# Cross-attention queries by a seven-product scheme, with the sample's padded queries kept for two chunks at a time

## The chip, the cores and the metric

The kernel runs on one core of a Trainium2 chip. The metric is the time of one execution on the device, in microseconds, as the median of several runs; smaller is better. The engines are named as in the profile: PE is the matrix engine (TensorE) and PEld its weight loads, DVE is VectorE, ACT is ScalarE, POOL is GpSimd, SP is the engine whose queue issues most of the transfers.

## The reference

One inference step of a decoder layer, for a prompt of 512 tokens and a sample group of 8 sequences with 8 tokens each, with the same weights; the model has 1024 channels, and all is float32.

```python
x = x + 0.5 * swiglu(rmsnorm(x, ffn1_norm), ffn1_w_gate, ffn1_w_up, ffn1_w_down)
h = rmsnorm(x, mix_norm);  u_lru, gate, u_pool = split(h @ w_in)
x = x + concat(gelu(gate) * rglru(conv(u_lru)), pool_mixer(u_pool)) @ w_out
x = x + cross_attend(rmsnorm(x, xattn_norm), mem_k, mem_v, xattn_wq, xattn_wo)
x = x + 0.5 * swiglu(rmsnorm(x, ffn2_norm), ffn2_w_gate, ffn2_w_up, ffn2_w_down)
y = rmsnorm(x, final_norm)

def cross_attend(h, k, v, wq, wo):                     # 4 heads of 256, 256 memory tokens
    q = (h @ wq).reshape(b, t, 4, 256)
    p = softmax(einsum('bthd,bmhd->bhtm', q, k) / 16)
    return einsum('bhtm,bmhd->bthd', p, v).reshape(b, t, 1024) @ wo
```

For the prompt, `mem_k` and `mem_v` are computed from the normed memory; for the sample they are inputs (a cache of 8 sequences x 256 tokens).

## The kernel before, in words

Activations lie transposed: 8 chunks (`DC`) of 128 channels, each 128 partitions x 576 tokens (512 of the prompt, 64 of the sample), in two halves of 288 (`HT`). Each float32 operand of a matmul is kept as a high part, rounded to the fp32r type by ScalarE (`split`, L182), and a low part, the rest, formed by VectorE (L185 or L187). A product takes three matmuls: high x high, high x low, low x high (`mm3`, all matmuls recorded at L139).

`project` takes one output chunk of 128 channels by all 8 input chunks: 8 x 3 x 2 halves = 48 matmuls of 288 columns. A weight panel (512 KB) goes through `panel`: a load into one of six `wr` buffers (L192), then the high and low part in one of four `wh` and four `wl` buffers each.

The feed-forward parts use another scheme, which the change brings to the queries. Two output chunks by two input chunks by two halves of the tokens form a 2 x 2 block product; it is done as seven block products (`product`, 12 matmuls of 288 columns each over four pairs of input chunks) on sums of weight blocks (`E`, `F`, `G`, `H` beside the plain `11`, `12`, `22`) and sums of the operand's blocks (`T1` to `T4` beside `N11`, `N21`, `N22`). `HalfNorm` keeps that operand: seven blocks of 288 for each pair of chunks, high and low; `sums` makes `T1` to `T3`, `last` makes `T4`. The accumulators `U`, `A`, `C` are read out between the products.

The stages around the change, in order:

- the output projection (`w_out`, tile `wo`): 8 panels; after each chunk the residual is added (L1250), and `nx.add` splits the new `x` into the operand `nx` of the queries and sums its squares. The squares of the memory tokens (`mem`) are summed meanwhile, and `mem` is normed and split into `mh`, `ml` (L1261).
- the memory keys (`mem_k`, tile `k`): 8 panels of 24 matmuls of 256 columns, results split into `kk` and sent out. The factor `r` of the norm is made after the third.
- the queries (`query`, tile `q`): 8 panels by `project`. `query_out` scales the result by `r` (L1278), splits the prompt's columns into `qq`, and copies the sample's columns to `z` (L1281), which is filled with zeros elsewhere, so that a matmul with it gives one head's scores at its rows.
- after every second chunk `sample_scores` multiplies the two chunks before with the cached keys: four loads of 512 KB (`ck`, L1300) into two `wh` and two `wl` buffers, and four small matmuls with each key (tile `ss`, L1302; each appears as two in the trace).
- then the values (`mem_v`), the last pair's sample scores, the softmax, and so on.

The order on each engine is made by a scheduler that takes the earliest ready instruction of the program; a buffer that comes free goes to the earliest tile that asks for it. Within the feed-forward parts (`"ff" in now`) the matmuls are chained in the program's order; in the rest they are not.

Of the kernel before, what the change touches and what calls it, by code (L numbers as in the profile page):

```python
# [16 lines left out]
P = 128  # L17
# [29 lines left out]
XH, HD = 4, 256  # L47
EPS = 1e-6


# [18 lines left out]
def hybrid_step(ctx, tc, a):  # L69
# [34 lines left out]
    def col(name, i=0):  # L104
        c = _C[name] + i
        return cst[:, c:c + 1]
# [10 lines left out]
    neg = const.tile([P, 2, DC], F32, name="neg")  # L117
    for i, name in enumerate(("g1", "g2")):
        v.tensor_scalar(neg[:, i, :], cst[:, _C[name]:_C[name] + DC], -1.0, None, op0=ALU.mult)

    def ncol(name, i=0):
        return neg[:, ("g1", "g2").index(name), i:i + 1]

# [5 lines left out]

    chain, latest = [None], [None]  # L130

# [5 lines left out]
    def mm(*args, **kw):  # L137

        i = te.matmul(*args, **kw)  # L139
# [1082 lines left out]

    nx = Norm("gx", "nx", now["r1"])
    xp = begin("xa")
    if True:
        def xtemp(n, name):
            return xp.tile([P, n], F32, tag="q", bufs=3, name=name)

        mem = xp.tile([P, DC, ML], F32, tag="B8", bufs=3, name="mem")
        nc.sync.dma_start(mem, a["memT"])  # L1230
        macc = xp.tile([P, ML], F32, name="macc")

        def mem_square(j):
            if j == 0:
                s.activation(macc, mem[:, j, :], AF.Square)
            else:
                sq = rows.tile([P, ML], F32, tag="sq", name="msq")
                s.activation(sq, mem[:, j, :], AF.Square)
                v.tensor_add(macc, macc, sq)

        wos = []
        for j in range(DC):
            wos.append((bank(f"wo{j}"), panel(a["w_out"][j], DC, P, "o", freed if j else None)))

            project(*wos[j], yy, range(LC, DC), last=False)
            if j < 2:
                continue
            for i in range(3) if j == 2 else (j,):
                project(*wos[i], yy, range(LC), first=False)
                v.tensor_add(halves(x[:, i, :]), wos[i][0][:, :, :HT], halves(x[:, i, :]))  # L1250
                nx.add(i)
            for i in range(3 * j - 6, min(3 * j - 3, DC)):
                mem_square(i)
            background()
            if j == 5:
                mq = row_factor([macc], "mem", wos[j][0][:, 1, :], ML)
            if j == 6:
                mr = spread(mq, "mem", ML)
                mh, ml = (xp.tile([P, DC, ML], F32R, tag="B8", bufs=3, name=f"m{q}") for q in "hl")
                for i in range(DC):  # L1260
                    v.scalar_tensor_tensor(out=mem[:, i, :], in0=mem[:, i, :], scalar=col("gk", i), in1=mr,  # L1261
                                           op0=ALU.mult, op1=ALU.mult)
                    split(mh[:, i, :], ml[:, i, :], mem[:, i, :])
# [6 lines left out]
        qs = {}  # L1270
# [5 lines left out]
        def query_out(j):  # L1276
            q = xtemp(T, f"q{j}")
            v.tensor_mul(halves(q), qs[j][:, :, :HT], halves(r))  # L1278
            split(qq[0][:, j, :TP], qq[1][:, j, :TP], q[:, :TP])
            h = j // 2  # L1280
            v.tensor_copy(z[:, :, j, h * ST:(h + 1) * ST], q[:, TP:].rearrange("p (b k) -> p b k", k=ST))  # L1281

        def mem_k(j):
# [5 lines left out]
            split(kk[:, 0, j, :], kk[:, 1, j, :], ps[:, 0, :ML])  # L1289
            o = xtemp(ML, f"ko{j}")  # L1290
            s.copy(o, ps[:, 0, :ML])
            nc.scalar.dma_start(a["o_k"][:, j, :], o)
            return ps

        def sample_scores(*js):

            for j in js:
                for g in range(2):
                    t = wp.tile([P, 4, ML], F32, tag=("wh", "wl")[g], name=f"ck{g}{j}")
                    nc.sync.dma_start(t, a["ck"][g, j])  # L1300
                    for b in range(4):
                        te.matmul(sps[b * 32:(b + 1) * 32, g, :ML], lhsT=z[:, 4 * g + b, j, :], rhs=t[:, b, :],  # L1302
                                      start=j == 0, stop=j == DC - 1)
# [12 lines left out]

        vv = now["r1"].tile([P, 2, 2, XH * HD], F32R, tag="A", bufs=2, name="vv")
        at = now["r1"].tile([P, DC * T], F32, tag="A", bufs=2, name="at")
        prob = [at[:, i * 4 * ML:(i + 1) * 4 * ML].rearrange("p (t n) -> p t n", n=ML) for i in range(2)]
        c0 = 8 * ML  # L1320
        pst = at[:, c0:c0 + 2 * ML].rearrange("p (g n) -> p g n", n=ML)
        pss = at[:, c0 + 2 * ML:c0 + 4 * ML].rearrange("p (g m n) -> p g m n", g=2, m=2)
        so = [at[:, c0 + (4 + i) * HD:c0 + (5 + i) * HD] for i in range(4)]

        def mem_v(h):
# [106 lines left out]
        mem_v(0)()  # L1432
        sample_scores(DC - 2, DC - 1)
        softmax(pst, sps[:, :, :ML], 2, "s")
# [32 lines left out]
        first[0] = None  # L1467
        end("xa")
        n2 = HalfNorm("g2", "n2", begin("s2"))
# [35 lines left out]
def _inputs(i):  # L1505
# [105 lines left out]
```

## Time and profile before

| | |
|---|---|
| median of 3 runs | 1124.35 us (1122.2 to 1124.86) |
| profiled execution, first to last instruction | 1120.1 us; no other time is given for it |
| TensorE busy, granted clock | 1104.7 us (99%), 0.997 |
| VectorE busy | 859.0 us (77%) |
| ScalarE busy | 669.7 us (60%) |
| queries, from the first q matmul to the last | 556.08 to 613.43 us |

Matmuls are pipelined and the row's mean duration of one is longer than their spacing, so the time of a group is read from the chain of waits: its rows are start, length, engine and tile, and number of instructions, in us. A row of a group of instructions is: line, engine, operation, output <- inputs, shapes, count | busy us, mean ns | idle time of the engine just before, and what ended it. A row of a stretch of time is: from:to, length, then for PE, PEld, DVE, ACT and POOL the busy us and the count of instructions, then the granted clock, the share of the DMA engines and GB/s.

### The profile page before, as it was taken

The page shows a single profiled execution, that of the slowest core. Times are in us where ns is not written, and L with a number is a line of the kernel's source. Part 1 is how long each engine was busy: PE and PEld are TensorE (multiplying, and loading weights), DVE is VectorE, ACT ScalarE, POOL GpSimd, SP SyncE. Part 2 cuts the span into 40 slices and gives each one's busy share as a digit, 9 for nine tenths or more (in the row PEclk, how much of TensorE's full clock was granted, in tenths as well). Part 3 has the DMA queues.
Part 4 walks back from the last instruction along what each step waited for, and adds up shares of the span by engine and source line. Part 5 has one row for each costly group of instructions (what it writes and reads, how often), then busy time and mean ns, then how long its engine had stood idle before and what let it go on. Part 6 is the DMA issues. An engine that isn't in the chain of part 4 may idle for free.

```text
span 1120.1 us, 21943 instructions
## 1 busy us (share of the span) xinstructions
PE 1104.7 (99%) x8430; PEld 1087.3 (97%) x8430; DVE 859.0 (77%) x1535; ACT 669.7 (60%) x1262; POOL 191.9 (17%) x232
## 2 busy tenths in 40 slices
PE   8999999999999999999999999999999999999997
PEld 8999999999999999999999889999999999999996
DVE  7899888889865878977733666779879888787754
ACT  8566666666664645765712455446667666666554
POOL 0012222221221024422000000000222222222111
PEclk9999999999999999999999999999999999999998
DMA  9457777776766656567656862233786777877652
GB/s 327 112 132 177 156 161 166 168 174 147 165 142 141 196 150 135 118 187 168 194 202 211 302 202 85 76 98 76 166 183 150 184 171 164 187 156 164 143 111 85
DMA packets 95257, 180.15 MB, mean 161 GB/s; under 512 B 9968, under 2 KB 47856, under 8 KB 95024
## 3 DMA queue, kind: packets, MB, share of 16 engines
q1 hardware_dynamic: 61024, 124.68, 35.0%
q0 software_dynamic: 31472, 51.65, 28.4%
q10 hardware_dynamic: 2656, 2.41, 0.7%
q8 instruction: 66, 1.08, 0.4%
q14 instruction: 39, 0.32, 0.1%
HBM read 140.87 MB, written 13.20 MB: 138 GB/s over the span
## 4 chain that ended last, share of the span: by engine, by line
PE 93%; DVE 3%; DMA 2%; issue 1%; ACT 1%; SPq 0%; POOL 0%; POOLq 0%; DVEq 0%; ACTq 0%
PE pu L139 22%; PE pc L139 10%; PE dU L139 9%; PE pd L139 6%; PE pa L139 5%; PE xo L139 5%; PE q L139 5%; PE wo L139 5%; PE pg L139 3%; PE in_l L139 2%; PE in_p L139 2%; PE in_g L139 2%; PE dA L139 2%; PE dD L139 2%; PE dC L139 2%; PE k L139 2%
## 5 line engine op out<-in xcount | busy, mean ns | idle before, releaser
L465 POOL DMA_DIRECT2D r<-f_gu x39 | 35.0, 897 | 425.3 <-DVE r L462 261.5
L182 ACT CAST dh<-td 128x512 fp32r<-128x512 f32 x96 | 59.3, 618 | 30.9 <-PE dA L139 12.2
L139 PE MATMUL dU<-ph,dh 128*128 128x288 f32 x256 | 75.7, 296 | 0.7 <-ACT add L651 0.7
L139 PE MATMUL dU<-ph,dl 128*128 128x288 f32 x256 | 75.4, 295 | 0.0
L139 PE MATMUL dU<-pl,dh 128*128 128x288 f32 x256 | 75.4, 295 | 0.0
L185 DVE TENSOR_TENSOR dl<-td,dh 128x512 fp32r<-128x512 f32 x96 | 64.6, 685 | 10.2 <-ACT dh L182 10.0
L185 DVE TENSOR_TENSOR wl_e<-r,wh_e 128x1024 fp32r<-128x1024 f32 x39 | 47.6, 1222 | 27.1 <-ACT wh_e L182 27.1
L667 POOL DMA_DIRECT2D x<-add_e x32 | 38.9, 1215 | 146.2 <-ACT add_e L651 43.5
L182 ACT CAST wh_g<-r 128x1024 fp32r<-128x1024 f32 x39 | 41.0, 1051 | 26.8 <-DVE r L481 14.1
L694 POOL DMA_DIRECT2D x<-add x32 | 31.3, 980 | 135.9 <-ACT add L651 91.0
L185 DVE TENSOR_TENSOR wl_h<-r,wh_h 128x1024 fp32r<-128x1024 f32 x39 | 47.6, 1220 | 3.0 <-ACT wh_h L182 3.0
L139 PEld LDWEIGHTS dU<-ph,dh 128*128 128x128 f32 x256 | 48.1, 188 | 1.2 <-ACT add L651 1.2
L139 PEld LDWEIGHTS dU<-ph,dl 128*128 128x128 f32 x256 | 48.2, 188 | 0.0
L139 PEld LDWEIGHTS dU<-pl,dh 128*128 128x128 f32 x256 | 48.1, 188 | 0.0
L185 DVE TENSOR_TENSOR wl_g<-r,wh_g 128x1024 fp32r<-128x1024 f32 x39 | 47.6, 1221 | 0.3 <-ACT wh_g L182 0.3
L182 ACT CAST wh_h<-r 128x1024 fp32r<-128x1024 f32 x39 | 40.9, 1049 | 10.3 <-PE pu L139 7.2
L182 ACT CAST wh_e<-r 128x1024 fp32r<-128x1024 f32 x39 | 41.1, 1053 | 0.6 <-PE pg L139 0.6
L875 ACT ACTIVATE g<-g 128x576 f32<-128x576 f32 x39 | 26.6, 683 | 24.1 <-DVE g L874 22.4
L701 POOL DMA_DIRECT2D x<-add x32 | 37.5, 1171 | 1.0 <-ACT add L651 0.8
L182 ACT CAST ph<-g 128x576 fp32r<-128x576 f32 (+1 forms) x39 | 22.9, 588 | 18.9 <-DVE g L581 10.5
L1278 DVE TENSOR_TENSOR q<-q,rstd_nx 128x576 f32<-128x576 f32 x8 | 6.1, 758 | 36.6 <-PE q L139 36.6
L651 ACT ACTIVATE add<-dU 128x288 f32<-128x288 f32 x64 | 26.2, 409 | 11.8 <-PE dU L139 11.8
(574 smaller groups left out, 4565.8 us busy)
## 6 DMA issues: line engine op xcount, KB each, us to landing
x<-add POOLq DMA_DIRECT2D x80, 288.0 KB, 5.8
r<-f_gu SPq DMA_DIRECT2D x39, 512.0 KB, 4.2
r<-f_gu SPq DMA_DIRECT2D x78, 256.0 KB, 3.6
td<-f_d SPq DMA_DIRECT2D x80, 128.0 KB, 4.9
r<-f_gu POOLq DMA_DIRECT2D x39, 256.0 KB, 4.6
x<-add_e POOLq DMA_DIRECT2D x32, 288.0 KB, 4.6
dsum<-f_d POOLq DMA_DIRECT2D x32, 256.0 KB, 5.1
ck<-ck SPq DMA_DIRECT2D x16, 512.0 KB, 5.2
```

The costliest lines, as they stand in the source:

```text
L139: i = te.matmul(*args, **kw)
L182: i = cast[0] = s.copy(hi, src)
L185: return v.tensor_tensor(out=lo, in0=src, in1=f(hi), op=ALU.subtract)
L465: nc.gpsimd.dma_start(r0[:, 0], wgu[f - plain, :, 3], accum_op=ALU.add)
L651: taken[0] = s.activation(dst, src, AF.Copy, scale=0.5 * sign)
L667: nc.gpsimd.dma_start(x[:, j:j + 2, HT:], t, accum_op=ALU.add)
L694: nc.gpsimd.dma_start(x[:, 2 * (i % NQ), :], t, accum_op=ALU.add)
L701: nc.gpsimd.dma_start(x[:, 2 * (i % NQ) + 1, :], t, accum_op=ALU.add)
L875: silu = s.activation(g, g, AF.Silu, scale=-1.0)
L1278: v.tensor_mul(halves(q), qs[j][:, :, :HT], halves(r))
```

## The change

The query projection is done by the seven-product scheme, in four passes (`query(p)`), each for two output chunks. Its operand `nx` becomes a `HalfNorm`; two of its four tiles lie in the space of the mixer's operand (`spare`), two in a new pool `xl`. The sums of the first two pairs of chunks are made in the output projection, those of the other two in the memory keys, as are `last` and the first weight sums (`prepare_q(0, "e")`, then `"g"`). The raw weights of a pass take three `wr` buffers (`load_q`), the two halves of the memory two more until they are split, and each `halves_sums` one. The sample's keys are loaded into `wr` buffers too, but for the last pair of chunks. `z` holds two chunks and is cleared in each pass. The matmuls of the passes, those of the sample's scores among them, are chained in the program's order (`pinned`). The weights are laid out on the host as in the feed-forward parts (`wqs`).

The diff, cut to its core:

```diff
+NEG = {"g1": 0, "g2": 1, "gx": 0}
...
-        if "ff" in now:
+        if "ff" in now or pinned[0]:
...
-        def __init__(self, gain, name, pool, acc=True):
+        def __init__(self, gain, name, pool, acc=True, tiles=None):
             self.gain, self.name = gain, name
-            self.xx = [[pool.tile([P, 2, 7, HT], F32R, tag="S", bufs=4, name=f"{name}{q}{i}") for i in range(2)]
+            self.xx = tiles or [[pool.tile([P, 2, 7, HT], F32R, tag="S", bufs=4, name=f"{name}{q}{i}") for i in range(2)]
...
-    nx = Norm("gx", "nx", now["r1"])
-    xp = begin("xa")
+    negate("gx")
+    xl, xp = begin("xl"), begin("xa")
...
+    spare = [now["r1"].tile([P, DC * T], F32R, tag="A", bufs=2, name=f"nx{i}0") for i in "hl"]
+    nx = HalfNorm("gx", "nx", None, tiles=[
+        [q[:, :14 * HT].rearrange("p (a b n) -> p a b n", a=2, b=7),
+         xl.tile([P, 4096], F32R, tag="S", bufs=2, name=f"nx{i}1")[:, :14 * HT].rearrange(
+             "p (a b n) -> p a b n", a=2, b=7)] for i, q in zip("hl", spare)])
...
+        memh = [wp.tile([P, DC // 2, ML], F32, tag="wr", bufs=WRB, name=f"mem{i}") for i in range(2)]
+        mem = [memh[i // 4][:, i % 4, :] for i in range(DC)]
+        for i in range(2):
+            nc.sync.dma_start(memh[i], a["memT"][:, 4 * i:4 * i + 4, :])
...
+        def halves_sums(i):
+            t = wp.tile([P, 2, KP, P], F32, tag="wr", bufs=WRB, name=f"t_nx{i}").rearrange("p a k n -> p (a k n)")
+            nx.sums(i, t[:, :3 * HT].rearrange("p (a n) -> p a n", a=3))
...
+                if i in (1, 3):
+                    halves_sums(i // 2)
...
-        z = xp.tile([P, NB, DC, 4 * ST], F32, name="z")
-        nc.gpsimd.memset(z, 0.0)
...
-        def query(j):
-            qs[j] = bank(f"q{j}")
-            project(qs[j], panel(a["wq"][j], DC, P, "q"), nx.xx)
...
-        def sample_scores(*js):
+        def sample_scores(js, **kw):
 
             for j in js:
-                for g in range(2):
-                    t = wp.tile([P, 4, ML], F32, tag=("wh", "wl")[g], name=f"ck{g}{j}")
+                for g, t in enumerate(keys(j, **kw)):
                     nc.sync.dma_start(t, a["ck"][g, j])
                     for b in range(4):
-                        te.matmul(sps[b * 32:(b + 1) * 32, g, :ML], lhsT=z[:, 4 * g + b, j, :], rhs=t[:, b, :],
-                                      start=j == 0, stop=j == DC - 1)
+                        mm(sps[b * 32:(b + 1) * 32, g, :ML], lhsT=z[:, 4 * g + b, j % 2, :],
+                                  rhs=t[:, b, :], start=j == 0, stop=j == DC - 1)
+        def keys(j, tags=("wr", "wr")):
+            return [wp.tile([P, 4, ML], F32, tag=tag, bufs=WRB if tag == "wr" else WSB, name=f"ck{g}{j}")
+                    for g, tag in enumerate(tags)]
+        raws, W = {}, {}
+        def load_q(p):
+            if p < KP:
+                r0, r1 = (wp.tile([P, 2, KP, P], F32, tag="wr", bufs=WRB, name=f"q{i}_{p}") for i in "01")
+                r2 = wp.tile([P, KP, P], F32, tag="wr", bufs=WRB, name=f"q2_{p}")
+                nc.sync.dma_start(r0, a["wqs"][p, :, 0:2])
+                nc.sync.dma_start(r2, a["wqs"][p, :, 3])
+                nc.sync.dma_start(r1[:, 0], a["wqs"][p, :, 2])
+                raws[p] = r0, r1, r2
+        def pair_of(src, nm_):
+            w = [wp.tile([P, 2, KP, P], F32R, tag=tag, name=f"{tag}_q{nm_}") for tag in ("wh", "wl")]
+            split(*w, src)
+            return [lambda q, k, i=i: w[q][:, i, k, :] for i in range(2)]
+        def prepare_q(p, what):
+            if p >= KP:
+                return
+            r0, r1, r2 = raws[p]
+            w = W.setdefault(p, {})
+            if what == "e":
+                v.tensor_add(r1[:, 1], r0[:, 0], r0[:, 1])
+                v.tensor_add(r0[:, 0], r0[:, 0], r2)
+                w["E"], w["11"] = pair_of(r0, "e")
+            elif what == "g":
+                v.tensor_add(r0[:, 1], r0[:, 1], r0[:, 0])
+                v.tensor_add(r0[:, 0], r0[:, 1], r1[:, 0])
+                w["G"], w["F"] = pair_of(r0, "g")
+            elif what == "h":
+                w["12"], w["H"] = pair_of(r1, "h")
+            else:
+                t = [wp.tile([P, KP, P], F32R, tag=tag, name=f"{tag}_q22") for tag in ("wh", "wl")]
+                split(*t, r2)
+                w["22"] = lambda q, k: t[q][:, k, :]
+                del raws[p]
+        def query_out(q, j):
+            split(qq[0][:, j, :TP], qq[1][:, j, :TP], q[:, :TP])
+            h = j // 2
+            v.tensor_copy(z[:, :, j % 2, h * ST:(h + 1) * ST], q[:, TP:].rearrange("p (b k) -> p b k", k=ST))
+        def query(p):
+            w = W[p]
+            t0, t1 = bank(f"qu{p}"), bank(f"qc{p}")
+            U, A, C = t0[:, 0, :HT], t0[:, 1, :HT], t1[:, 0, :HT]
+            q0, q1 = (xtemp(T, f"q{2 * p + e}") for e in range(2))
+            product(U, w["11"], nx, N11, True)
+            s.copy(q0[:, :HT], U)
+            prepare_q(p, "h")
+            product(C, w["E"], nx, T1, True)
+            s.copy(q1[:, HT:], C)
+            prepare_q(p, "22")
+            if p:
+                sample_scores((2 * p - 2, 2 * p - 1))
+            product(U, w["F"], nx, T2, False)
+            s.copy(q0[:, HT:], U)
+            product(A, w["12"], nx, N21, True)
+            v.tensor_add(q0[:, :HT], A, q0[:, :HT])
+            product(U, w["H"], nx, T3, False)
+            v.tensor_add(q1[:, HT:], U, q1[:, HT:])
+            product(C, w["G"], nx, N22, False)
+            v.tensor_add(q0[:, HT:], C, q0[:, HT:])
+            nc.gpsimd.memset(z, 0.0)
+            v.scalar_tensor_tensor(out=q0, in0=q0, scalar=-1.0, in1=r, op0=ALU.mult, op1=ALU.mult)
+            query_out(q0, 2 * p)
+            prepare_q(p + 1, "e")
+            prepare_q(p + 1, "g")
+            product(U, w["22"], nx, T4, False)
+            v.tensor_mul(q1[:, HT:], q1[:, HT:], r[:, HT:])
+            v.tensor_mul(q1[:, :HT], U, r[:, :HT])
+            query_out(q1, 2 * p + 1)
+            load_q(p + 2)
 
         for j in range(DC):
             mem_k(j)
             if j == 2:
                 r = nx.rstd_wide()
+            if j in (1, 3):
+                halves_sums(j // 2 + 2)
+            if j == 4:
+                load_q(0)
+            if j == 6:
+                prepare_q(0, "e")
+            if j > 5:
...
+                nx.last(j - 6, halves(rows.tile([P, T], F32, tag="sq", name=f"t4_nx{j}")))
+        load_q(1)
+        prepare_q(0, "g")
         sps = bank("ss")
-        for j in range(DC):
-            query(j)
-            query_out(j)
-            if j and j % 2 == 0:
-                sample_scores(j - 2, j - 1)
+        z = rows.tile([P, T], F32, tag="acc", bufs=1, name="z")[:, :2 * NB * 4 * ST].rearrange(
+            "p (b e k) -> p b e k", b=NB, e=2)
+        pinned[0], chain[0] = True, latest[0]
+        for p in range(KP):
+            query(p)
+        pinned[0] = False
...
-            pp = xp.tile([P, 2, 2, TP], F32R, tag="B8", bufs=3, name=f"pp{h}")
+            pp = xl.tile([P, 2, 2, TP], F32R, tag="S", bufs=2, name=f"pp{h}")
...
-        sample_scores(DC - 2, DC - 1)
+        sample_scores((DC - 2, DC - 1), tags=("wh", "wl"))
+        at = now["r1"].tile([P, DC * T], F32, tag="A", bufs=2, name="at")
...
-    out["wq"] = panels(l0["xattn_wq"])
+    q = panels(l0["xattn_wq"]).reshape(KP, 2, P, KP, 2, P).transpose(0, 2, 1, 4, 3, 5)
+    out["wqs"] = q.reshape(KP, P, 4, KP, P)[:, :, [2, 0, 1, 3]]
```

More of the change, by code (lines that the diff above doesn't have):

```diff
@@ L117, in hybrid_step, with negate @@
     neg = const.tile([P, 2, DC], F32, name="neg")
-    for i, name in enumerate(("g1", "g2")):
-        v.tensor_scalar(neg[:, i, :], cst[:, _C[name]:_C[name] + DC], -1.0, None, op0=ALU.mult)
+    def negate(*names):
+        for name in names:
+            v.tensor_scalar(neg[:, NEG[name], :], cst[:, _C[name]:_C[name] + DC], -1.0, None, op0=ALU.mult)
+    negate("g1", "g2")
     def ncol(name, i=0):
-        return neg[:, ("g1", "g2").index(name), i:i + 1]
+        return neg[:, NEG[name], i:i + 1]
     s.activation(rows.tile([P, T], F32, tag="acc", bufs=1, name="table")[:, :1], ones, AF.Sqrt)
     begin("ff", space=PSUM)
-    chain, latest = [None], [None]
+    chain, latest, pinned = [None], [None], [False]
     def after_(i, j):
@@ L1289, in mem_k @@
             split(kk[:, 0, j, :], kk[:, 1, j, :], ps[:, 0, :ML])
-            o = xtemp(ML, f"ko{j}")
+            o = (xp if j % 2 else rows).tile([P, ML], F32, tag="macc" if j % 2 else f"rstd{ML}", bufs=1, name=f"ko{j}")
             s.copy(o, ps[:, 0, :ML])
@@ L1432, in hybrid_step @@
         mem_v(0)()
-        sample_scores(DC - 2, DC - 1)
+        sample_scores((DC - 2, DC - 1), tags=("wh", "wl"))
+        at = now["r1"].tile([P, DC * T], F32, tag="A", bufs=2, name="at")
+        prob = [at[:, i * 4 * ML:(i + 1) * 4 * ML].rearrange("p (t n) -> p t n", n=ML) for i in range(2)]
+        c0 = 8 * ML
+        pst = at[:, c0:c0 + 2 * ML].rearrange("p (g n) -> p g n", n=ML)
+        pss = at[:, c0 + 2 * ML:c0 + 4 * ML].rearrange("p (g m n) -> p g m n", g=2, m=2)
+        so = [at[:, c0 + (4 + i) * HD:c0 + (5 + i) * HD] for i in range(4)]
         softmax(pst, sps[:, :, :ML], 2, "s")
@@ L1467, in hybrid_step @@
         first[0] = None
-        end("xa")
+        end("xa", "xl")
         n2 = HalfNorm("g2", "n2", begin("s2"))
```

29 lines of the change are left out of this document (7 added, 22 removed).

## The prediction

> **What bounds the kernel now.** I read the page's first part, then the chain that ended last, then the windows of the stages that the change touches, then the rows of the instructions that it adds, and last the queue of loads.
>
> ```profile
> span 1120.1 us, 21943 instructions
> PE 1104.7 (99%) x8430; PEld 1087.3 (97%) x8430; DVE 859.0 (77%) x1535; ACT 669.7 (60%) x1262; POOL 191.9 (17%) x232
> ```
>
> TensorE is busy for the whole span, so time is won only where matmuls go, and lost where TensorE has to wait. The chain of waits around the query stage is nothing but PE:
>
> ```profile
> 451.20 6.40 PE in_g L139 x48
> ...
> 542.40 13.68 PE k L139 x114
> 556.08 19.20 PE q L139 x144
> 575.27 1.86 PE ss L1302 x32
> 577.13 12.99 PE q L139 x96
> 590.12 1.86 PE ss L1302 x32
> 591.99 12.99 PE q L139 x96
> 604.98 1.86 PE ss L1302 x32
> 606.84 6.59 PE q L139 x48
> ```
>
> The queries (`q`) are 144+96+96+48 = 384 matmuls, at 6.40 us for 48 (133 ns each). The scores of the sample (`ss`) sit between them in blocks of 1.86 us and wait for nothing.
>
> ```profile
> 480.04:556.08 76.04, 76.04 (x590) 75.80 (x590) 60.79 (x98) 50.02 (x80) 14.32 (x17) 1.00 0.66 167
> 556.08:613.43 57.35, 57.35 (x482) 54.08 (x482) 19.35 (x29) 12.14 (x17) 0.00 (x0) 1.00 0.62 217
> ```
>
> These rows are the output projection with the memory keys, and the query stage (columns: PE, PEld, DVE, ACT, POOL busy, clock, DMA share, GB/s). In the query stage VectorE is free two thirds of the time; in the stage ahead of it four fifths are taken.
>
> **The change part by part.**
>
> *Seven products for eight.* A pair of output chunks takes seven products of 12 matmuls, four pairs 28 products = 336 matmuls. The feed-forward part already runs this scheme, with the same tile shape:
>
> ```profile
> 311.46 1.58 PE pu L139 x12
> ...
> 316.20 1.59 PE pu L139 x12
> ```
>
> 28 x 1.59 = 44.5 us against 8 x 6.40 = 51.2: TensorE is relieved of **6.7 us**. Nothing else is on the path there, so all of it is won, if nothing new waits.
>
> *VectorE's work inside the query stage.* The rows (same shapes, feed-forward stretch; `nxl` and `q` from the stages above):
>
> ```profile
> L185 DVE TENSOR_TENSOR wl_g<-r,wh_g 128x1024 fp32r<-128x1024 f32 x16 | 19.5, 1221 | 0.3 <-ACT wh_g L182 0.3
> L480 DVE TENSOR_TENSOR r<-r 128x512 f32<-128x512 f32 x16 | 10.9, 684 | 0.0
> L185 DVE TENSOR_TENSOR wl<-r,wh 128x512 fp32r<-128x512 f32 x15 | 10.3, 685 | 0.0
> L881 DVE TENSOR_TENSOR e<-pu,e 128x288 f32<-128x288 f32 x15 | 6.8, 452 | 0.6 <-PE pu L139 0.3
> L187 DVE SCALAR_TENSOR_TENSOR nxl<-x,cst,nxh 128x576 fp32r<-128x576 f32 x7 | 5.7, 813 | 2.7 <-ACT nxh L186 2.7
> L1281 DVE COPY z<-q x8: 188/189/195, 563.4 to 614.3; 128x64 f32<-128x64 f32 x8
> ```
>
> Per pair: four sums of 512 (2.74), three low parts of 1024 (3.66) and one of 512 (0.69), three additions and two scalings of 288 from PSUM (2.26), one scaling of 576 (0.81), two low parts of the query (1.37), two copies to `z` (0.38): 11.9 us, against 7 x 1.59 + 1.86 = 13.0 us of TensorE, or 92%. That is as full as the feed-forward part, where TensorE does not wait:
>
> ```profile
> 780.00:820.00 40.00, 40.00 (x304) 40.00 (x303) 36.77 (x64) 28.08 (x57) 8.73 (x9) 1.00 0.69 157
> ```
>
> So I cost the steady load at nothing; cover gone, the excess over 13.0 would show. ScalarE has some 6 us of casts and copies per pair and is no bound. The four `memset`s of `z` go to POOL, idle in this stage; each may start when the scores ahead of product F have been read, some 6 us before the copies that need it. SP issues three weight loads a pair for two; at about 0.3 us an issue (rows below) they cost nothing.
>
> *The operand's sums.* Each of the four `halves_sums` is one scale-and-add, two subtractions and a low part of 864; each of the two `last` is two scale-and-subtracts and a subtraction and low part of 576:
>
> ```profile
> L352 DVE SCALAR_TENSOR_TENSOR t_n<-x,neg,b_n 128x288 f32<-128x288 f32 x3 | 1.5, 511 | 0.0
> L353 DVE TENSOR_TENSOR t_n<-b_n,t_n 128x288 f32<-128x288 f32 x3 | 1.4, 452 | 0.0
> L185 DVE TENSOR_TENSOR n2l<-t_n,n2h 128x864 fp32r<-128x864 f32 x3 | 3.2, 1058 | 2.9 <-ACT n2h L182 2.9
> L373 DVE TENSOR_TENSOR t_pl<-t_pl,n2l 128x576 f32<-128x576 f32 x1 | 0.8, 750 | 0.0
> L185 DVE TENSOR_TENSOR wl_q<-wr_q,wh_q 128x1024 fp32r<-128x1024 f32 x3 | 3.6, 1219 | 0.0
> ```
>
> 0.511 + 2 x 0.452 + 1.058 = 2.47 us and 2 x 0.511 + 2 x 0.75 = 2.52 us. Two of the sums fall into the output projection, where VectorE idles 11 us; hidden. The other two, both `last`, and the first pair's weights (`e` and `g`: 2 x (2 x 0.684 + 1.221) = 5.18) fall into the memory keys: 4.95 + 5.05 + 5.18 = 15.2 us, less the three `wl_q` that go (3.6): 11.6 us more. What is free there:
>
> ```profile
> 525.40:532.20 6.80, 6.80 (x54) 6.80 (x54) 6.73 (x14) 4.24 (x10) 1.06 (x1) 1.00 0.58 119
> 532.20:538.00 5.80, 5.80 (x49) 5.63 (x48) 5.80 (x12) 4.50 (x9) 1.06 (x1) 1.00 0.49 60
> 538.00:544.00 6.00, 6.00 (x51) 5.96 (x50) 5.58 (x9) 4.73 (x9) 0.00 (x0) 1.00 0.89 278
> 544.00:550.00 6.00, 6.00 (x52) 6.00 (x51) 3.14 (x5) 5.82 (x9) 0.00 (x0) 1.00 0.47 145
> 550.00:556.00 6.00, 6.00 (x52) 6.00 (x51) 5.76 (x9) 3.72 (x8) 0.00 (x0) 1.00 0.73 189
> ```
>
> 30.6 us, of which VectorE is busy 27.0: 3.6 free. So 8.0 us of work is left when the queries should start. `g` is last in the order and is wanted by the third product, two products (3.2 us) later: TensorE waits 4.8 us, either there or for a low part of `wk` queued behind the sums. Some of the third sum may slip into idle time ahead of 525, so I take **4 us**. Ends: 0, if both `last` (5.05) run behind `g`; 8.4, if the 3.6 free us can't be filled.
>
> *The sample's keys.* This decides. Today a pair's four keys (512 KB each) go into the `wh`/`wl` buffers and are asked for one round ahead:
>
> ```profile
> 527.48 26.78 SPq L192 DMA_DIRECT2D wr_q<-wq  x8
> 555.46 0.33 SPq L192 DMA_DIRECT2D wr_v<-wv  x1
> ...
> 575.90 3.09 SPq L1300 DMA_DIRECT2D ck<-ck  x4
> 579.04 7.17 SPq L192 DMA_DIRECT2D wr_v<-wv  x2
> ```
>
> Loads go out in the program's order as buffers come free: the four keys issued at 575.90, while the scores of the pair before are read, serve the block at 590.12, 14 us later. After the change the keys share the six `wr` buffers with the raw weights, three buffers a pair. The third pair's weights are asked for at the end of the first pair, ahead of the keys, and take the three buffers that the first pair leaves. The second pair's own three come free when its splits are done: `g`, `h`, `22` in turn, and each of those waits for a `wh`/`wl` pair (four) that a product of the first pair must give up: H at -3.2, G at -1.6, 22 at 0 us (0 = start of the second pair). Cast (1.05) and low part (1.22; for `22` 0.62 and 0.69), with VectorE's evictions between, free them at about -0.5, 1.5 and 3. Only three: the third pair's `g` can't free one, since it needs the buffers of product G, which stands behind the scores in the pinned order. So **the fourth key is loaded into the first key's buffer, after that key's matmuls, with TensorE standing still.** A load's price:
>
> ```profile
> DMA to landing us min/median/max: 3.4/5.2/7.7
> ...
> DMA to landing us min/median/max: 3.5/4.6/5.3
> ```
>
> The first line is `ck` (issued four at a time), the second `wq` (one at a time, as the keys now will be): I take 4.6. Keys 1 to 3 land at 4.1, 6.1, 7.6; key 4 goes out at 4.1 + 0.47 (a quarter of 1.86) and lands at 9.2; the block ends at 9.7 in place of 3.18 + 1.86 = 5.0: a wait of 4.6 us. In the third pair it is the same, since the fourth pair's weights take what the second's keys leave. In the fourth pair no weights follow: three keys are early and the last has the first freed buffer, so about 0. The last keys (6 and 7) keep `wh`/`wl`, behind a projection of 5.63 us. Sum **9.2 us**. Ends: with 3.4 us a load and every key but the last in time, 3.18 + 0.47 + 3.4 + 0.47 - 5.04 = 2.5 a pair, 5.0; with 5.3 a load, 6.0 a pair, 12.0.
>
> *The rest* (the memory in two `wr` halves, output tiles for the keys moved, `at` later) adds no work; two of six `wr` buffers less for the weight panels until 540 is in the upper end of the second term.
>
> **Sum:** -6.7 + 4 + 9.2 = +6.5 us on the span of 1120.1. The profile gives no other time for that execution; the median of the runs, 1124.35, lies 4.25 above its span, and I carry that over: 1120.1 + 4.25 + 6.5 = **1130.8 us**. About 0.3% (3.4 us) is what a measurement here can tell from no change.
>
> **The rivals.**
> *Faster.* The buffers are handed out otherwise than I read, and the fourth key goes out before the second pair's first product is through; VectorE's rest is taken up by the four-deep buffers. Then -6.7 alone: 1117.7. For it: 92% of VectorE stalls nothing in the feed-forward part. Against: there no keys share the `wr` buffers, and today's queue keeps the program's order.
> *No change.* VectorE's 4 us is hidden and the keys cost only their lower end: -6.7 + 5.0 = -1.7, 1122.7.
> *Far slower.* The keys' waits run together and the clock falls. The trace shows it only at the end, with TensorE almost idle:
>
> ```profile
> 1112.00:1120.00 8.00, 0.71 (x4) 0.52 (x4) 2.57 (x8) 0.37 (x1) 1.27 (x1) 0.60 0.40 137
> ```
>
> My four waits per block are 0.9 to 1.5 us with matmuls between, so I add nothing; in one piece, at 0.6 of the clock for as long again as each wait of 4.6, it is 2 x 4.6 x 0.4/0.6 = 6 us more: 1137. [...]
>
> **How the numbers follow.** Forecast (both waits come) 0.58, its own range 1127.8 (no change's bound) to 1138.0 (-6.7 + 8.4 + 12.0); no change 0.20; faster 0.17; far slower 0.05. Slower is 0.58 + 0.05 = 0.63. The range runs from 1119.5, which leaves out most of the faster case, to 1137, which leaves out the top of the slow ones: about 2 in 10 outside.
>
> **What would show it.** Right: `q` tiles with 336 matmuls at 132 ns; in the chain, DMA pieces `ck` of 4 to 5 us in the second and third pair, one `ck` load issued behind the first `ss` matmuls of its own block; VectorE full from 525 to the third product of the first pair, and a PE wait on `wl_q` or `wl_k` of some 4 us. Wrong: `ss` blocks of 1.86 us in one piece with all keys landed, or no PE wait ahead of the first F.

## The result and the profile after

The changed kernel takes 1167.35 us (median of 4 runs, 1167.21 to 1169.22); beside it the kernel before took 1124.15 us (4 runs). The ratio is 1.0392, interval 1.0377 to 1.0407: 43 us slower. The forecast of 1130.8 us had the direction; the time lies 30 us above its range.

The first part of the page of the kernel after:

```profile
span 1165.5 us, 21983 instructions
PE 1115.1 (96%) x8382; PEld 1090.8 (94%) x8382; DVE 896.0 (77%) x1600; ACT 688.6 (59%) x1296; POOL 192.2 (16%) x235
```

TensorE has 48 matmuls less (384 - 336, as forecast), yet its busy time rose by 10.4 us. The clock tells why; first, where the time went. Windows from the first matmul of a stage to the first of the next (output projection, memory keys, queries up to the first prompt score), before:

```profile
479.90:532.10 52.20, 52.20 (x395) 52.17 (x394) 40.55 (x67) 31.21 (x48) 13.26 (x16) 1.00 0.67 166
532.10:555.90 23.80, 23.80 (x197) 23.59 (x197) 20.39 (x32) 18.77 (x33) 1.06 (x1) 1.00 0.64 168
555.90:620.90 65.00, 65.00 (x563) 60.67 (x561) 23.40 (x35) 15.53 (x21) 0.00 (x0) 1.00 0.63 215
```

and after:

```profile
480.20:550.70 70.50, 58.71 (x394) 57.52 (x393) 44.92 (x77) 33.99 (x54) 11.65 (x15) 0.88 0.48 114
550.70:587.40 36.70, 27.05 (x199) 26.11 (x198) 31.10 (x51) 23.84 (x40) 1.58 (x2) 0.86 0.51 144
587.40:665.20 77.80, 64.16 (x506) 54.87 (x504) 44.21 (x72) 26.81 (x41) 1.58 (x3) 0.96 0.57 190
```

The stages grew by 18.3, 12.9 and 12.8 us, together 44.0 of the span's 45.4. The largest part is in the output projection, whose matmuls the change did not touch. What TensorE waits for from 475 to 720 us (us in total, times, longest), after:

```profile
PE wo L144 <- ACT wh_o L187: 11.4, 2, 6.8
PE ss L144 <- DMA ck<-ck: 7.7, 7, 1.9
PE k L144 <- ACT wh_k L187: 7.5, 2, 5.9
PE qu L144 <- DVE q L1371: 3.1, 3, 1.8
PE qu L144 <- ACT q L1369: 1.5, 3, 0.5
```

*Output projection.* TensorE stands twice, 4.59 and 6.85 us, for ScalarE's cast of a panel. These are ScalarE's casts ahead of the end of the first wait, at 504.16 us (timeline: start, length, instruction):

```profile
500.70 0.91 ACT L187 CAST nxh<-t_nx 128x864 fp32r<-128x864 f32 x1 [1.29 <-DVE t_nx L358]
...
503.08 1.03 ACT L187 CAST wh_o<-wr_o 128x1024 fp32r<-128x1024 f32 x1
```

The cast of the panel stands behind a cast of the operand's sums (`t_nx`), and that waits for a chunk of `x` that TensorE has just finished; 17.5 us later, at 518.22, the same comes again. So TensorE has run out of panels before the next is cast. SyncE's timeline, before and then after, shows the panels' loads:

```profile
414.87 59.66 SPq L192 DMA_DIRECT2D wr_o<-w_out  x8
...
490.40 0.35 SPq L1219 DMA_DIRECT2D o_small<-small  x1
```

```profile
415.20 6.60 SPq L1242 DMA_DIRECT2D mem<-memT  x2
430.90 16.24 SPq L197 DMA_DIRECT2D wr_o<-w_out  x3
488.83 0.35 SPq L1224 DMA_DIRECT2D o_small<-small  x1
489.28 31.30 SPq L197 DMA_DIRECT2D wr_o<-w_out  x5
```

Before, all eight were asked for ahead of the store of `o_small`, by 474.5 us; after, three. Three things could be behind it: the memory in two `wr` buffers, the store that holds up the queue, or the sums tile `t_nx`, which each `halves_sums` takes from `wr`.

*The clock.* After the waits it is halved (windows of the kernel after; the column before the DMA share):

```profile
504.10:510.10 6.00, 5.80 (x22) 5.45 (x23) 1.81 (x4) 0.42 (x2) 0.00 (x0) 0.50 0.64 208
...
535.00:541.00 6.00, 6.00 (x48) 5.98 (x47) 3.58 (x6) 3.95 (x5) 1.62 (x2) 1.00 0.63 148
```

There are 22 matmuls in 6 us where 48 go at full clock: the first wait costs 3 us more in the 6 us behind it, and so does the second (25 matmuls in the 6.6 us from 520.70 on, at 0.50). 11.4 of waits and some 6.4 of half clock are 17.8 of the 18.3 us, and TensorE's busy time grows with it.

*Query stage.* The chain of waits from the first block of keys on:

```profile
603.07 1.58 PE qc L144 x12
604.65 0.61 PE ss L144 x8
...
605.28 5.07 DMA ck<-ck
...
611.47 2.45 PE qu L144 x12
...
613.94 0.41 ACT q L1369
...
614.39 1.87 PE qu L144 x12
...
616.35 0.47 DVE q L1371
...
616.87 1.85 PE qu L144 x12
```

A product that waits for nothing takes the forecast 1.58 us. The load of the fourth key takes 5.07 us behind the first key's matmuls (4.64 in the next pair), as forecast, and the block takes 6.82 us (6.39 in the next pair) in place of 1.86; in the fourth pair it is in one piece of 1.9. Within the block TensorE's waits are in pieces: 1.62, 1.70 and 0.30 us for the second, third and fourth key, then 0.95, 1.91 and 0.61.

Not forecast are three things behind the block. Product `F` takes 2.45 us (2.66 in the next pair): the clock is halved there too, for some 3.4 us behind the second block (0.50 from 629.90 to 633.30). Product `12` waits for ScalarE's copy of `U` (L1369, 1.5 us in three pairs), and product `H` for VectorE's reading of `A` (L1371, 3.1 us). `U` and `A` are the two halves of one tile, and the matmuls of the one wait for the readers of the other.

### The profile page after: what moved, and what is told of

Read it like the earlier page. It is cut to its first block, busy times and chain, and to the rows that moved or that the text cites. A ratio compares the mean times of both kernels' runs of the same rounds, so it can differ in the third digit from the quotient of the medians.

```text
span 1165.5 us, 21983 instructions
## 1 busy us (share of the span) xinstructions
PE 1115.1 (96%) x8382; PEld 1090.8 (94%) x8382; DVE 896.0 (77%) x1600; ACT 688.6 (59%) x1296; POOL 192.2 (16%) x235
## 4 chain that ended last, share of the span: by engine, by line
PE 85%; DVE 7%; DMA 4%; issue 2%; ACT 2%; SPq 0%; POOL 0%; POOLq 0%; DVEq 0%; ACTq 0%
PE pu L144 21%; PE pc L144 10%; PE dU L144 8%; PE pd L144 6%; PE pa L144 5%; PE xo L144 4%; PE wo L144 4%; PE pg L144 3%; PE in_l L144 2%; PE in_p L144 2%; PE qu L144 2%; PE in_g L144 2%; PE dC L144 2%; PE dA L144 2%; PE dD L144 2%
## 5 line engine op out<-in xcount | busy, mean ns | idle before, releaser
L144 PE MATMUL wo<-yh,wh_o 128*128 128x288 f32 x128 | 30.0, 318 | 11.4 <-ACT wh_o L187 11.4
L144 PEld LDWEIGHTS wo<-yh,wh_o 128*128 128x128 f32 x128 | 22.6, 208 | 11.9 <-ACT wh_o L187 11.9
```

## The experiments

Theories: A, the memory's two `wr` buffers starve the panels; B, SyncE stands at `o_small`; C, VectorE and ScalarE are overloaded by the sums; A2, formed after the first two runs, the place of the sums tiles in line for `wr`; D, the tile that `U` and `A` share; E, the fourth key. The edits up to e8_all are against the changed kernel (1167.35 us), the later ones against the run that is named; a run without an interval is one execution.

**e1_mem**

```diff
-        memh = [wp.tile([P, DC // 2, ML], F32, tag="wr", bufs=WRB, name=f"mem{i}") for i in range(2)]
-        mem = [memh[i // 4][:, i % 4, :] for i in range(DC)]
+        memt = xp.tile([P, 2, DC, ML], F32, tag="kk", name="mem")
+        mem = [memt[:, 0, i, :] for i in range(DC)]
```

> The changed kernel, with the memory no longer in two `wr` buffers but in the space that the projected keys take later, so that all six `wr` buffers serve the weight panels during the output projection. Theory A (the panels of the output projection and of the key projection came late because two of six buffers held the memory): the output projection's stage, 52.2 us before and 70.5 after the change, goes back to 52 to 58, the key projection's stage from 36.7 to 25 to 33, the whole to 1138 to 1153 us (from 1167.3). Rival B (SyncE stands at the store of `o_small` until 488.8 and the buffers don't matter): the stage stays over 64 us, the whole 1160 to 1168. Rival C (VectorE and ScalarE are overloaded by the sums of the operand's halves): no stage changes by over 2 us.

Measured 1170.12 us; the output projection 68.8 us (from 479.7 to 548.5), the keys' stage 36.3. Theory A falls: the panels were still asked for in the order three, `o_small`, five. The whole is 2.8 us longer because the query stage takes 82.7 us in this execution, at a clock of 0.86 (0.96 in the kernel after); e6_memsums comes back to that.

**e2_small**

```diff
-    nc.sync.dma_start(a["o_small"], small)
+    nc.gpsimd.dma_start(a["o_small"], small)
```

> The changed kernel, with the store of `o_small` issued by GpSimd in place of SyncE, the memory still in two `wr` buffers. Theory A (buffers): at most three panels' loads come earlier, those that SyncE issued at 489.3 to 490.2; as they were cast at 503.1 behind waits for TensorE, the stage loses 0 to 8 us of its 70.5, the whole is 1159 to 1168. Rival B (SyncE's standing at the store is the cause): the stage returns to 52 to 56 us, the whole to 1148 to 1153.

Measured 1169.58 us. SyncE no longer stands at the store, and the fourth and fifth panel are asked for from 471.95 us (SyncE's timeline):

```profile
471.95 4.56 SPq L197 DMA_DIRECT2D wr_o<-w_out  x2
```

yet ScalarE casts them when it did before, behind the sums (its timeline in this run):

```profile
501.24 0.91 ACT L187 CAST nxh<-t_nx 128x864 fp32r<-128x864 f32 x1 [1.30 <-DVE t_nx L358]
503.61 1.03 ACT L187 CAST wh_o<-wr_o 128x1024 fp32r<-128x1024 f32 x1
```

TensorE's wait for `wh_o` is again 11.4 us. Theory B falls, and the loads as such with it: a panel that landed some 27 us ahead (4.1 us from issue to landing in this run) is cast no earlier. What holds it is its place in ScalarE's order.

**e3_acc**

```diff
-            U, A, C = t0[:, 0, :HT], t0[:, 1, :HT], t1[:, 0, :HT]
+            U, C, A = t0[:, 0, :HT], t1[:, 0, :HT], t1[:, 1, :HT]
```

> The changed kernel, with the product of `12` accumulated in the tile of the even chunk's second half (`C`) in place of the tile of `U`, so that no product waits for a read of the other half of its tile. Theory D (the shared tile holds TensorE up twice in each pair by about 2.2 us): the query stage falls from 77.8 to 68 to 72 us, the whole to 1157 to 1162. Rival (TensorE would have stood for something else there, the drain of its own pipeline or VectorE): under 2 us, 1165 to 1168.

Measured 1157.74 us. The query stage, 77.8 us in the kernel after:

```profile
585.10:656.30 71.20, 63.90 (x514) 55.57 (x513) 44.48 (x72) 26.91 (x42) 1.58 (x3) 0.93 0.63 212
```

Theory D holds: of the 9.6 us, 6.6 are in this stage, and no wait of a `qu` product for a read is left among TensorE's waits. The other 3 us lie in stages that the edit doesn't touch, and with one execution nothing more can be said of them.

**e4_key**

```diff
             if p:
                 sample_scores((2 * p - 2, 2 * p - 1))
+                load_q(p + 1)
...
-            load_q(p + 2)
```

> The changed kernel, with the loads of the next pair's sums of weights issued right behind the loads of the keys, not ahead of them at the end of the pair before. Theory E (the fourth key's load stands behind the pair's loads and their buffers, 4.6 to 5.0 us in the second and third pair): both waits go, the query stage falls by 8 to 10 us to 68 to 70, the whole to 1157 to 1160, if the next pair's sums still come in time. Rival F (the loads are then late for the sums of the next pair, so that the wait stands at the first product of the pair): the waits at the keys go and 2 to 4 us per pair come back, the whole 1160 to 1168. Rival G (the keys wait for their buffers, not behind the loads): no change, 1165 to 1169.

Measured 1157.42 us; the query stage 70.0 us. TensorE's waits there:

```profile
PE qu L144 <- ACT q L1370: 4.5, 3, 2.1
PE qu L144 <- DVE q L1372: 2.2, 3, 0.9
...
PE ss L144 <- DMA ck<-ck: 0.3, 1, 0.3
```

The keys' wait of 7.7 us is 0.3: theory E holds, and not for the fourth key alone: all three late keys stood behind the next pair's loads. 7.8 us of the stage go. Part of F, the rival in the expectation, came too: the loads are late for the next pair's sums, ScalarE's cast waits for these (3.5 us in the second pair), and the copy of `U` stands behind that cast, so that TensorE waits 4.5 us for copies where it was 1.5.

**e5_sums**

```diff
-            t = wp.tile([P, 2, KP, P], F32, tag="wr", bufs=WRB, name=f"t_nx{i}").rearrange("p a k n -> p (a k n)")
-            nx.sums(i, t[:, :3 * HT].rearrange("p (a n) -> p a n", a=3))
+            if i < 2:
+                t = memt[:, 1].rearrange("p k n -> p (k n)")[:, i * 3 * HT:(i + 1) * 3 * HT]
+            else:
+                t = now["r2"].tile([P, 3 * HT], F32, tag="A", bufs=2, name=f"t_nx{i}")
+            nx.sums(i, t.rearrange("p (a n) -> p a n", a=3))
```

(`memt` is a tile in the space of `kk`, as in e1_mem, here without the memory. The query operand `qq`, whose space the last two sums take first, is allocated behind them.)

> The changed kernel, with the four tiles of the operand's sums out of the `wr` buffers (the first two in the space that the projected keys take later, the last two in that of the query operand); the memory stays in two `wr` buffers. Theory A2 (a sums tile is handed out of the same six buffers in program order, between the panels of the output projection, so every later panel's load is issued only when the sums begin to be written; in SyncE's order the store of `o_small` then stands ahead of five panels, and ScalarE's order has their casts late): the output projection's stage, 70.5 us, goes back to 52 to 56, the whole to 1144 to 1153. Theory A (the memory's two buffers): the stage stays over 62 us, the whole over 1158. Rival C (VectorE and ScalarE are overloaded by the sums themselves): under 3 us.

Measured 1149.71 us, 17.6 less. Here are the output projection and the memory keys:

```profile
481.80:533.90 52.10, 52.10 (x394) 52.08 (x393) 44.46 (x75) 34.67 (x54) 11.48 (x15) 1.00 0.60 141
533.90:567.50 33.60, 26.69 (x198) 25.91 (x198) 27.88 (x48) 21.16 (x38) 1.58 (x2) 0.90 0.43 122
```

The output projection is what it was before the change, though the memory still holds two `wr` buffers and the sums are still formed there (VectorE 44.5 us busy for 40.6). ScalarE's cast of a panel now stands ahead of the sums:

```profile
500.99 1.05 ACT L187 CAST wh_o<-wr_o 128x1024 fp32r<-128x1024 f32 x1
502.69 0.92 ACT L187 CAST nxh<-t_nx 128x864 fp32r<-128x864 f32 x1 [0.66 <-DVE t_nx L358]
```

Theory A2 is shown, for these 18 us; A and C are out there. The tile of the sums is asked for, in the program's order, ahead of the fourth panel. Buffers of `wr` are handed out in that order, so no later panel gets its place on any engine until the sums are placed.

**e6_memsums** (e5_sums and e1_mem together)

> As the run before, and the memory too out of `wr`, so that all six buffers serve weights. If the memory's buffers cost something once the sums no longer block (the key projection's panels and the first pair's loads find four buffers), the key projection's stage falls to 24 to 30 us from 30 to 36 and the whole to 1136 to 1146; if they cost nothing, within 1.5 us of the run before.

Measured 1152.15 us, 2.4 more than e5_sums, which neither side expected. The keys' stage gains 3.8 us, but the query stage goes from 78.9 to 84.8. Here are two windows, the keys' stage and a stretch of the queries:

```profile
534.30:564.10 29.80, 25.78 (x198) 25.19 (x197) 25.58 (x45) 21.21 (x38) 1.58 (x2) 0.94 0.40 110
...
590.00:601.00 11.00, 9.89 (x40) 9.20 (x40) 2.50 (x6) 1.45 (x2) 0.00 (x0) 0.50 0.09 28
```

Behind a block of keys with waits of 1.42, 1.94 and 0.53 us the clock was halved for over 11 us here; in the kernel after, behind pieces much like these, for 3.4 us. It isn't bound to this edit: e2_small, whose edit doesn't touch the queries, shows both in one execution. Its chain of waits, product `F` behind the first block (waits of 1.46, 2.09 and 0.16 us), then three products behind the second (1.44, 1.44 and 0.61 us):

```profile
611.99 2.31 PE qu L144 x12
...
631.87 3.19 PE qu L144 x12
...
635.54 3.26 PE qu L144 x12
...
639.40 3.25 PE qu L144 x12
```

The second block costs some 4 us more than the first for no cause in the edit, so the 2.4 us by which e6_memsums is longer say nothing of the memory's place.

**e7_sums_acc_key** (e5_sums, e3_acc and e4_key together)

> The changed kernel with the sums out of `wr`, the product of `12` in the tile of `C`, and the next pair's loads behind the keys (three edits; the memory stays in `wr`). If the three causes are apart, their gains add: 1167.3 less 15 to 18 (sums), 9.6 (shared tile) and 9.9 (keys) is 1129.8 to 1132.8 us. If one hides another (VectorE or the loads as a common bound in the query stage), 1136 or more.

Measured 1134.37 us: 33.0 less, where the three gains sum to 37.1. The missing 4 us are about what e3_acc and e4_key had gained outside the query stage (3.0 and 2.1). Inside it the causes are apart: the stage takes 64.1 us, 14.8 less than in e5_sums, for 6.6 and 7.8 alone.

**e8_all** (all four edits)

> All four edits: sums and memory out of `wr`, the product of `12` in the tile of `C`, the next pair's loads behind the keys. By the sum of the terms 1118 to 1130 us; with the stage of the queries at 57.6 to 60 us (44.5 of products, 7.4 of keys' matmuls, 5.6 of value matmuls that fall in it) and the key projection at 24 to 28. Against the kernel before that is a tie or a gain of up to 6 us: the saved matmuls, 6.7 us, are all that the change can bring.

Measured 1131.37 us, 1.4 over the range. The query stage takes 63.4 us, the memory keys:

```profile
534.80:565.60 30.80, 26.77 (x198) 26.22 (x198) 26.54 (x46) 21.04 (x38) 1.59 (x2) 0.91 0.38 107
```

36 of the 43 us are accounted for. The keys' stage is still 7 us longer than before.

**e9_order** (e8_all, and:)

```diff
-            if j == 2:
+            if j == 3:
                 r = nx.rstd_wide()
...
-            if j == 4:
-                load_q(0)
             if j == 6:
+                ahead[7] = panel(a["wk"][7], DC, P, "k")
+                load_q(0)
                 prepare_q(0, "e")
...
-                if i in (1, 3):
+                if i in (1, 3, 5):
                     halves_sums(i // 2)
...
+            first[0] = held          # casts of the next pair behind the copy of U
             prepare_q(p + 1, "e")
             prepare_q(p + 1, "g")
+            first[0] = None
```

> The four edits of the run before (1131.4 us), and the order of the key projection's stage mended: the last weight panel is loaded ahead of the first pair's sums of weights, the sums of the third pair of chunks are formed in the output projection, the row factors one product later, and ScalarE's casts for the next pair stand behind the copy of `U` in the pair before. In the run before, the key stage took 30.8 us against 23.8 in the kernel before, with TensorE standing 2.1 us for a panel and 1.9 us for the row factors; the query stage 63.4 us against a sum of its matmuls of 57.7. If these orders are what is left: key stage 25 to 28, query stage 60 to 62, the whole 1122 to 1128 us. If VectorE's work is the bound there (26.5 us busy of 30.8), the key stage stays over 29 and the whole over 1128.

Measured 1129.61 us (ratio to the kernel before 1.0059, 1.0042 to 1.0076), 1.6 above the range. The keys' stage and the first pair, in the trace of the longest of its four runs (1132.72 us):

```profile
533.90:557.70 23.80, 23.80 (x199) 23.63 (x198) 22.30 (x39) 18.74 (x34) 1.59 (x2) 1.00 0.42 106
557.70:576.10 18.40, 14.33 (x86) 13.86 (x85) 14.21 (x25) 8.34 (x13) 0.00 (x0) 0.81 0.34 108
```

The stage is back at its 23.8 us, but the first pair, 11.1 us of products, takes 18.4: TensorE waits 4.1 us for the cast and the low part of `g`, which is late by what `last` puts ahead of it, and then its matmuls start 240 ns apart for some 6 us, from 565.6 to 571.6, for 133 at full clock. Those waits are the forecast's second term, in its place and size.

**e10_pool** (e9_order with the sums of raw weights by GpSimd)

```diff
-                v.tensor_add(r1[:, 1], r0[:, 0], r0[:, 1])
+                nc.gpsimd.tensor_add(r1[:, 1], r0[:, 0], r0[:, 1])
...
```

> As e9_order, with the sixteen sums of raw weight blocks of the four pairs formed by GpSimd in place of VectorE (0.68 us each there, 2.7 us per pair). If VectorE still limits the key stage or the first pair: 1 to 4 us less than e9_order, to 1118 to 1126 us. If it doesn't: no change; if GpSimd is so slow that the first products of a pair wait for its sums (over about 2.5 us each): 2 to 8 us more.

Measured 1133.45 us (1.0101, 1.0086 to 1.0116), slower than e9_order. GpSimd's additions (group by line, 500 to 640 us) took 1.3 to 1.6 us each where VectorE takes 0.68 to 0.69, in series with the load. One of its four groups:

```profile
L1338 POOL TENSOR_TENSOR q<-q 128x512 f32<-128x512 f32 x4 | 6.4, 1588 | 26.0 <-DMA q<-wqs 13.1 <-PE qu L144 8.9 <-DVE wl_k L190 4.0
```

**e11_late** (e9_order without the hold, `last` moved behind the first pair's `g` and `h`)

```diff
             prepare_q(p, "h")
+            if p == 0:
+                for i in range(2):
+                    nx.last(i, halves(rows.tile([P, T], F32, tag="acc", bufs=1, name=f"t4_nx{i}")))
```

> As e9_order (1129.6 us; its key stage 23.7 us as in the kernel before, but its first pair of queries 18.4 us against 11.1 us of matmuls), with the last two sums of the operand (2.9 us of VectorE each) moved behind the first pair's own sums `g` and the split of `h`, and without the hold on ScalarE's casts for the next pair. If VectorE's order at the first pair is what is left there: the first pair takes 11.5 to 14 us, the whole 1122 to 1127 us. If VectorE's total is the bound: the wait moves to the last product of the pair, which needs those sums, and the whole stays at 1127 to 1131 us.

Measured 1127.68 us (1.0041, 1.0028 to 1.0054), 0.7 above the first range; the first pair takes 13.8 us, and no product waits for `last`. It was an order there, not VectorE's total.

**e12_late_hold** (the same with the hold)

> As e11_late, with the hold on ScalarE's casts kept. In e8_all, without it, the product of `H` stood 1.5 us in all for the copy of `U`; in e9_order, with it, those waits went and the keys' loads came 3.8 us late in all. If the hold delays the release of the weight buffers and so the keys: 1 to 3 us slower than e11_late. If the two have nothing to do with each other: up to 1.5 us faster.

Measured 1126.71 us (1.0033, 1.0021 to 1.0045); no worse, so the hold isn't what makes the keys late. TensorE waits 1.31, 1.19 and 1.48 us for them in the three pairs.

**e13_keys_f and e14_keys_a** (e12_late_hold, the keys and `load_q` behind `F`, and behind `12`)

```diff
-            if p:
-                sample_scores((2 * p - 2, 2 * p - 1))
-                load_q(p + 1)
             product(U, w["F"], nx, T2, False)
             held = s.copy(q0[:, HT:], U)
             product(A, w["12"], nx, N21, True)
             v.tensor_add(q0[:, :HT], A, q0[:, :HT])
+            if p:
+                sample_scores((2 * p - 2, 2 * p - 1))
+                load_q(p + 1)
```

> As e12_late_hold (1126.7 us), with the keys' matmuls and the next pair's loads one product later in the pair, behind the product of `F` (1.59 us). If what is left is the wait for the fourth key's buffer (1.31, 1.19 and 1.48 us in the profile of e12_late_hold), all three waits go and the whole is 4 us less, 1122 to 1124 us, a tie with the kernel before. If the buffers are handed on so that the wait moves along: 1126 to 1128 us.

> As e12_late_hold, with the keys' matmuls and the next pair's loads two products later, behind the product of `12`. As e13_keys_f if the buffer is the cause (1122 to 1124 us); 1 to 4 us above it if the next pair's loads, now 3.2 us later, come late for its sums and casts.

Measured 1125.59 us (1.0026, 1.0017 to 1.0035) and 1125.18 us (1.0020, 1.0011 to 1.0029), both above the 1122 to 1124 that were expected. In e14_keys_a the keys' waits are gone, but only 1.5 us with them, which is within what the runs vary by. Its query stage:

```profile
555.70:621.30 65.60, 60.84 (x506) 54.17 (x505) 47.78 (x80) 27.45 (x43) 2.10 (x4) 1.00 0.62 214
```

The two stages ahead are what they were before the change (52.1 and 23.8 us); this one is 65.6 us for 65.0, though it holds 6.7 us less of products. TensorE stands for 4.8 us of it, in pieces of at most 1.3 us. Its chain of waits, from the loads issued in the third pair on:

```profile
588.45 5.56 DMA q<-wqs
...
594.13 0.70 DVE q L1338
...
595.58 1.06 ACT wh_qe L187
596.66 1.23 DVE wl_qe L190
...
603.15 1.15 DVE wl_qh L190
...
604.93 6.01 DMA wr_v<-wv
```

It runs through no matmul. From load to load it is 16.5 us here (14.9 in the round before): a load waits for the buffer that a split gives back, lands after 5.56 us, and then sums, casts and splits follow one another. TensorE needs 13.0 us a pair. As far as this chain shows, that loop eats the saving; more `wr` buffers would test it, and no run here has them.

The profiled span is 2.6 us longer than before, and only 0.6 of that lies in the query stage. Another 0.9 us is a wait of TensorE for ScalarE's cast `wh_s` ahead of the second feed-forward part. It is in every run with the edit of e5_sums, and neither in the kernel before nor in the kernel after: it comes with that edit, not with the change.

## Why the prediction was wrong

- **The products, -6.7 us: right.** 1.58 to 1.59 us for each that runs without a wait at full clock.
- **The fourth key, +9.2: right, in mechanism and size.** The blocks take 6.82 and 6.39 us for 1.86, which is 9.5 us more, in the second and third pair and not in the fourth; e4_key shows the cause.
- **VectorE ahead of the queries, +4: right in kind, hidden in the result.** In the kernel after it is overlaid by late panels. With the order mended it cost 7.3 us (e9_order, 18.4 - 11.1; 4.1 of them waits, most of the rest half clock) and, with `last` behind `g`, 1.7 to 2.7: inside the forecast's ends of 0 and 8.4.
- **"The rest … adds no work": the step that failed.** It weighed the new use of `wr` as work and as a number of buffers, and put it in the upper end of another term. The sums tiles cost by their place, not by their work, which e5_sums still does in the same stage. Standing in line for `wr` between the panels, they pushed casts and loads of panels behind themselves: 18.3 us in the output projection (e5_sums), 3.1 in the memory keys. The memory's two buffers, which the forecast named, cost 3.8 us in the memory keys and nothing in the output projection. The change's text shows where `halves_sums` allocates, and the row for the panels' loads (eight asked for ahead) shows how far ahead they ran; I quoted the loads of the query stage and not these.
- **The steady load "at nothing": failed too.** The forecast compared VectorE's 11.9 us with TensorE's 13.0 a pair and with the feed-forward part. Two things differ there. `U` and `A` share a tile, which the diff shows: 6.6 us (e3_acc). And a load stands in series with VectorE's work, since the keys share the six buffers: 14.9 and 16.5 us a pair in the loop above. The first is shown; that the second limits the stage is argued from one chain.
- **The clock: failed too.** "My four waits … so I add nothing" did not hold; that short pieces cost nothing was the author's estimate. In the kernel after, half clock followed the pieces at the keys in both blocks (0.30 to 1.70 us, then 0.61 to 1.91) and lengthened product `F` by 0.9 and 1.1 us; in e6_memsums, behind pieces of 0.53 to 1.94 us, it lasted over 11 us. The larger part of the half clock came in the output projection, behind waits of 4.59 and 6.85 us in one piece, and cost some 3 us behind each. The far slower case has 4.6 x 0.4/0.6 = 3.1 us for a wait of 4.6 in one piece: its clock of 0.6 is that of the row from 1112 us on, its length, as long again as the wait, the author's estimate. Measured were 0.50 for 6.0 and 6.6 us.
- The ledger: 18.3 + 12.9 - 6.7 + 9.5 + 6.6 is 40.6 of the 45.4 us of span. The rest, 4.8 us, is 3.4 in the query stage (12.8 - 9.4), of which the half clock behind the two key blocks makes 1.9, and 1.4 outside the three stages.

The fastest version run, e14_keys_a (its interval overlaps that of e13_keys_f), is still 0.2% slower than the kernel before: with the errors of placing mended, no gain of the seven products is left to measure here.

## What to carry to other kernels

A tile put into a shared pool of buffers took a place in a line here, not only a buffer (18.3 us in the output projection, e5_sums): ask what is allocated behind it in the program, and whether that was running ahead. Two accumulators in one tile waited for each other's readers (6.6 us of the query stage, e3_acc). And VectorE's share of a stage says little while its work stands in series with a load: add up the loop from buffer to buffer, and compare that with what TensorE needs.

## What the runs showed of the hardware

- After a wait of 4.59 us TensorE ran at half clock for 6.0 us (240 ns a matmul for 133), after 6.85 us for 6.6 (kernel after).
- Half clock followed waits in pieces too, with bursts of the keys' matmuls between them: 3.4 us of it behind 0.95, 1.91 and 0.61 us (kernel after), over 11 us behind 1.42, 1.94 and 0.53 us (e6_memsums). In one execution of e2_small one product was lengthened behind the first block (2.31 us for 1.58) and three behind the second (3.19 to 3.26 us). What sets the length, no run here shows.
